# A decoder layer with product-key experts: half of the second-key one-hots on GpSimd, 16 more second-weight passes beside the first weights, a ranking in wider steps

## The chip, the core and the metric

The kernel runs on one core of a Trainium2 chip as one program. The metric is the device time of one execution in microseconds (us). A core has five engines that run their own instruction streams in order and wait for each other by semaphores: TensorE (PE in the profile; PEld is its weight load), VectorE (DVE), ScalarE (ACT), GpSimd (POOL) and SyncE (SP, which here only issues DMAs). DMAs are issued from SP, ACT and POOL, each with a queue of its own; the gathers by index come from POOL.

## What is computed

One layer of a decoder for a prompt of 512 tokens and 8 x 8 sample tokens, with a model width of 2048, in float32. The first half (conditioned norms, an input projection, a gated recurrence and a short convolution, an output projection) isn't touched by the change. The second half is a layer of 16384 single-neuron experts, chosen by product keys:

```python
q = (xb @ w_q).reshape(PEER_BLOCK, PEER_HEADS, 2, HALF_DIM)
sc = jnp.einsum('thpk,pnk->thpn', q, sub_keys)
v1, i1 = lax.top_k(sc[:, :, 0], PEER_TOPK)      # 16 best of 128 first keys
v2, i2 = lax.top_k(sc[:, :, 1], PEER_TOPK)      # 16 best of 128 second keys
cand = v1[..., :, None] + v2[..., None, :]      # 256 pairs
top, pos = lax.top_k(cand, PEER_TOPK)           # 16 of them per head
g = softmax(top)
act = gelu(einsum('td,thkd->thk', xb, expert_u[eidx])) * g
out = einsum('thk,thkd->td', act, expert_v[eidx])
```

With 8 heads each token picks 128 experts. `expert_u` holds the first weights, `expert_v` the second, 16384 rows of 2048 each.

## The kernel before, in words

Experts are grouped by their first key into 128 blocks of 128. A ranking orders the blocks by how often they are picked. For the prompt tokens, the 76 best ranked blocks (L) are computed densely: all 512 tokens against all 128 experts of a block on PE. Picks outside these blocks, and all picks of the sample tokens, are gathered row by row: a POOL DMA fetches 128 expert rows (one per partition, 1 MB) into one of five row buffers (seven in the second stage), and DVE makes one pass over it. A pass in the first-weight stage is a dot product (line 1310); in the second-weight stage it adds the row, weighted, to an accumulator (line 1337). There are 233 passes of the first kind (5 of them copies of token rows) and 228 of the second, in one order; a counter `gu` says how far the passes are, `gf` how far the fetches. Sample rows come first in both halves, as a tile of 64 full gathers; the five tiles of prompt tokens have slots that are left empty.

The work runs in two long stages after the projections.

The first-weight stage has 152 pieces (half a block each, 24 matmuls of 128x512, line 1451). All products are made from a rounded high half and the remainder: ACT makes `xhi` (line 931), POOL `xlo` (line 932), two pieces ahead. Between the pieces, a generator `steps1` (function `choice`) hands out the choosing of the last head, the resolving of indices, a second ranking of the blocks behind the 48th (`rank_rest`), and the sort of the tokens; each step carries a guessed cost, and a balance `spare` says how many are done per piece. When it ends, `steps2` makes the slot lists of one tile of tokens after the other, and gathers of that tile may follow. Alongside, dense weights are built: for each token a matrix of first key by second key, as a product of two one-hots on PE (line 1652, 8 matmuls per 4 tokens). DVE makes the one-hots of 8 tokens in one call (`g_pair`, line 1638: `op` is 128x8x128 for the second key, `wr` 128x8x76 for the first), reading the key row from PSUM; ACT scales each token's `op` by its weight (line 1646). `upto(n)` sets how many must be ready at a piece. `RATE[1]` passes are due per piece while `steps2` runs; then `gather_to` spreads what is left, so that `EARLY_V` passes of the second kind are done when the stage ends.

The second-weight stage has 76 steps of 48 matmuls (line 1471), each with 4 x 0.25 MB of second weights. Every four steps need dense weights (`gsb`, from `gd`) and activations (`actr`), loaded from ACT's queue, multiplied on DVE and split into halves `ahi`, `alo`. The remaining passes are spread over the first 69 steps in proportion to the room that PE's time leaves.

Both stages are recorded by hand in this order (a manual schedule), so the program text fixes each engine's order. PSUM banks of the kind "g" rotate between two: a score, a step of a ranking and a one-hot product that follow each other take turns on them.

Of the kernel before, what the change touches and what calls it, by code (L numbers as in the profile page):

```python
# [10 lines left out]
ALU = mybir.AluOpType  # L11
# [33 lines left out]
LATE = 1  # L45
PIECE = 5.5
BEHIND = 7.0
RATE = (1.0, 2.0)
PIECE_G = 6.9
HEADS_COUNTED = 4  # L50
RANKED = 48
# [1 line left out]
LAG = 4  # L53
FIRST_G = 6
PAIRS = 8
EARLY_V = 8
KEPT = 5
WEIGH = 2.8
PARTS = 2
# [25 lines left out]
def build(ctx, tc, A, O, dbg=None):  # L85
    nc = tc.nc
    V, S, PE, G = nc.vector, nc.scalar, nc.tensor, nc.gpsimd
# [17 lines left out]
    iota = const.tile([128, 128], F32, name="iota")  # L105
# [314 lines left out]
    t0 = c1.tile([128, KW], F32, name="t0")  # L420
# [19 lines left out]
    o = big.tile([128, KD, T], F32, name="o", tag="big")  # L440
# [419 lines left out]
    for i in range(RB):  # L860
        r, k = new_row(f"row0_{i}")
# [691 lines left out]
    late = list(range(QT))  # L1553
    it, stg, pair, puts = [], {}, {}, []

    def choice():
# [5 lines left out]
        picked, rest = iter(()), rank_rest()  # L1562
        yield None
        for a, z in enumerate(order):
            next(rest, None)
            if a and a + 1 < len(order):
                side[order[a + 1]] = score(h, order[a + 1])
            choose(h, side[z], z)
            yield 6.0
            if z == "S":  # L1570
                for _ in resolve("S", EARLY_S, HD // 2 - EARLY_S):
                    yield 4.0
                yield 1.5
                picked = pick_samples()
            yield next(picked, 0.0)
            yield next(picked, 0.0)
        soft = {}
        for z in late:
            for _ in resolve(z, HD - HB):
                yield 9.5  # L1580
            yield 5.5
            yield next(picked, 0.0)
            soft[z] = softmax(z)
            next(soft[z])
# [35 lines left out]
    gk = {}  # L1620
# [9 lines left out]
    def g_pair(b):  # L1630

        rg = pools["rg"]
        t0 = b * 4
        ops = rg.tile([128, 8, 128], F32, name=f"op{b}", tag="op", bufs=PAIRS // 2)
        wr = rg.tile([128, 8, L], F32, name=f"wr{b}", tag="wr", bufs=PAIRS // 2)
        for out, src, j in ((ops, gk["o"], 1), (wr, gk["w"], 0)):
            n = src.shape[-1]
            V.tensor_tensor(out, src[:, None, :].to_broadcast([128, 8, n]),  # L1638
                            it[j][:, t0:t0 + 8, None].to_broadcast([128, 8, n]), op=ALU.is_equal)
        pair[b], pair[b + 1] = (ops, wr, 0), (ops, wr, 4)  # L1640

    def g_scale(b):

        ops, wr, j0 = pair[b]
        for j in range(4):
            S.activation(ops[:, j0 + j, :], ops[:, j0 + j, :], AF.Copy, scale=it[2][:, b * 4 + j:b * 4 + j + 1])  # L1646

    def g_mm(b):
# [26 lines left out]
    spare, due_g = -BEHIND, 0.0  # L1675
# [14 lines left out]
    for n in range(NU2):  # L1690
# [7 lines left out]
        if R1 is not None:  # L1698
            put(2)
            g_one(n)  # L1700
            if not gk:
                g_start()
            elif gm[0] < min(upto(n), gm[1] + PAIRS - 1):
                g_pair(gm[0])
                gm[0] += 2
                spare -= 2.2
            while gm[2] < gm[3]:
                g_scale(gm[2])
                gm[2] += 1
            gm[3], gm[4] = gm[4], gm[0]  # L1710
# [14 lines left out]
        if not even:  # L1725
# [4 lines left out]
            if since is not None and n > since + 2:  # L1730
                due_g += RATE[R1 is not None] + (0.7 if waits and spare > 4.5 else 0.0)
            g0 = gu[0]
# [5 lines left out]
            if waits:  # L1738
                spare = min(spare, 3.0)
# [62 lines left out]
    for m in range(M):  # L1802
        gi, q, bl, first, final = steps[m]
        n = NU2 + 2 * m
# [4 lines left out]
        for kq in range(KD // VQ):  # L1809
# [16 lines left out]
            k, pv = v_column(n, gi, q, bl, first, final, kq)  # L1826
# [33 lines left out]
    with tc.If(any_ > 0), tc.tile_pool(name="fb", bufs=1) as fp:  # L1860
        io1 = fp.tile([128, 128], F32, name="f_io1")
        V.tensor_scalar(io1, iota, 1.0, None, op0=ALU.add)
        for i, (p0, n, c) in enumerate(GT):
# [9 lines left out]
            w = kk[:, 1, :]  # L1873
# [9 lines left out]
            a = fp.tile([128, D], F32, name=f"f_a{i}", tag="a", bufs=1)  # L1883
# [105 lines left out]
```

## Time and profile before

| what | us |
|---|---|
| median of 3 runs | 3182.85 (3177.85 to 3182.97) |
| profiled execution | 3185.91 |
| its span, first to last instruction | 3184.1 |
| first-weight stage (first and last start of its matmuls) | 1183.7 to 2181.5 |
| second-weight stage | 2181.5 to 3159.1 |
| one-hots on DVE | 1518.5 to 2061.7 |
| PE, DVE, POOL, ACT busy | 3006.2, 2129.4, 1762.6, 1021.2 |

Busy shares say little over the whole span, since its stages differ; rows below are taken by stretch of time. A row of instruction groups reads: line, engine, operation, tiles, shapes, count, then busy time, mean duration in ns, and the idle time of that engine just before them, with what ended it. A row of waits reads: who waited, for whom, us in total, times, longest. In the DMA views a line of an issue ends with its count and the median us from issue to landing; a line of a queue has packets, MB and the share of the 16 DMA engines' time. A busy PE is not PE at its peak, since ends of matmuls are modelled.

### The profile page before, as it was taken

The page shows a single profiled execution, that of the slowest core. Times are in us where ns is not written, and L with a number is a line of the kernel's source. Part 1 is how long each engine was busy: PE and PEld are TensorE (multiplying, and loading weights), DVE is VectorE, ACT ScalarE, POOL GpSimd, SP SyncE. Part 2 cuts the span into 40 slices and gives each one's busy share as a digit, 9 for nine tenths or more (in the row PEclk, how much of TensorE's full clock was granted, in tenths as well). Part 3 has the DMA queues.
Part 4 walks back from the last instruction along what each step waited for, and adds up shares of the span by engine and source line. Part 5 has one row for each costly group of instructions (what it writes and reads, how often), then busy time and mean ns, then how long its engine had stood idle before and what let it go on. Part 6 is the DMA issues. An engine that isn't in the chain of part 4 may idle for free. (4 is left out here: it accounts for less than half of the span.)

```text
span 3184.1 us, 46037 instructions
## 1 busy us (share of the span) xinstructions
PE 3006.2 (94%) x16954; PEld 2550.9 (80%) x16954; DVE 2129.4 (67%) x3301; ACT 1021.2 (32%) x1619; POOL 1762.6 (55%) x1071
## 2 busy tenths in 40 slices
PE   6999999999999999999999999997999898989797
PEld 2788888889989997887888888875888676767576
DVE  3455521142246899987998999966577687769755
ACT  3244311122232232222656655622322121112122
POOL 2233333344334235667566666667888686878662
PEclk9999999999999999999999999998999999999898
DMA  9744566533332127889879999999999998899984
GB/s 394 279 138 137 178 214 216 205 122 131 128 118 102 68 81 258 309 305 391 311 309 368 420 369 409 403 367 379 381 400 406 381 340 324 326 363 364 368 305 146
DMA packets 292071, 892.40 MB, mean 280 GB/s; under 512 B 35776, under 2 KB 75584, under 8 KB 237664
## 3 DMA queue, kind: packets, MB, share of 16 engines
q0 software_dynamic: 67776, 435.61, 34.3%
q1 hardware_dynamic: 157152, 372.00, 32.5%
q10 hardware_dynamic: 66912, 81.81, 7.4%
q8 instruction: 134, 2.20, 0.3%
q14 instruction: 97, 0.79, 0.1%
HBM read 879.89 MB, written 64.71 MB: 297 GB/s over the span
## 5 line engine op out<-in xcount | busy, mean ns | idle before, releaser
L932 POOL TENSOR_TENSOR xlo<-raw,xhi 128x1024 fp32r<-128x1024 f32 x304 | 738.7, 2441 | 324.2 <-ACT xhi L931 233.1
L1337 DVE SCALAR_TENSOR_TENSOR accB<-v,dots,accB 128x2048 f32<-128x2048 f32 x216 | 508.2, 2353 | 214.3 <-DMA v<-v,rows 213.1
L931 ACT ACTIVATE xhi<-raw 128x1024 fp32r<-128x1024 f32 x304 | 318.3, 1058 | 883.7 <-PE pv L1471 251.7
L1310 DVE SCALAR_TENSOR_TENSOR u<-u,hT 128x2048 f32<-128x2048 f32 x228 | 515.3, 2281 | 98.6 <-DMA u<-u,rows 98.1
L1471 PE MATMUL pv<-ahi,xhi 128*128 128x512 f32 x1216 | 491.2, 404 | 62.1 <-ACT xhi L931 47.3
L1471 PE MATMUL pv<-ahi,xlo 128*128 128x512 f32 x1216 | 487.8, 401 | 14.6 <-POOL xlo L932 14.5
L1451 PE MATMUL pu<-hhi,xhi 128*128 128x512 f32 x1216 | 492.8, 405 | 3.7 <-ACT xhi L931 3.7
L1471 PE MATMUL pv<-alo,xhi 128*128 128x512 f32 x1216 | 488.7, 402 | 5.9 <-POOL alo L1426 5.9
L1451 PE MATMUL pu<-hhi,xlo 128*128 128x512 f32 x1216 | 480.6, 395 | 7.1 <-POOL xlo L932 7.1
L1451 PE MATMUL pu<-hlo,xhi 128*128 128x512 f32 x1216 | 478.9, 394 | 0.0
L1282 POOL DMA_INDIRECT u<-u,rows x228 | 232.0, 1018 | 231.1 <-DVE u L1310 171.5
L1471 PEld LDWEIGHTS pv<-ahi,xhi 128*128 128x128 f32 x1216 | 233.7, 192 | 124.8 <-ACT xhi L931 52.6
L1471 PEld LDWEIGHTS pv<-ahi,xlo 128*128 128x128 f32 x1216 | 233.1, 192 | 75.6 <-POOL xlo L932 21.2
L1471 PEld LDWEIGHTS pv<-alo,xhi 128*128 128x128 f32 x1216 | 233.2, 192 | 60.0 <-POOL alo L1426 7.6
L1282 POOL DMA_INDIRECT v<-v,rows x228 | 248.5, 1090 | 58.2 <-issue 37.3
L1451 PEld LDWEIGHTS pu<-hhi,xlo 128*128 128x128 f32 x1216 | 230.1, 189 | 62.0 <-POOL xlo L932 9.8
L1451 PEld LDWEIGHTS pu<-hhi,xhi 128*128 128x128 f32 x1216 | 230.6, 190 | 50.3 <-ACT xhi L931 4.5
L1451 PEld LDWEIGHTS pu<-hlo,xhi 128*128 128x128 f32 x1216 | 231.1, 190 | 46.1
L1646 ACT ACTIVATE op<-op,it 128x128 f32<-128x128 f32 x512 | 155.6, 389 | 31.6 <-DVE op L1638 31.2
L132 POOL TENSOR_TENSOR wlo_o<-raw_o,whi_o 128x1024 fp32r<-128x1024 f32 x32 | 77.5, 2423 | 119.9 <-ACT whi_o L130 119.9
L1652 PEld LDWEIGHTS gbank<-wr,op 128*128 128x128 f32 x1024 | 133.7, 191 | 12.6 <-ACT stg L1659 2.6
L132 POOL TENSOR_TENSOR wlo_q<-raw_q,whi_q 128x1024 fp32r<-128x1024 f32 x28 | 67.2, 2402 | 132.3 <-ACT whi_q L130 132.3
(515 smaller groups left out, 5542.9 us busy)
## 6 DMA issues: line engine op xcount, KB each, us to landing
wa<-w_ada SPq DMA_DIRECT2D x96, 1024.0 KB, 7.4
raw<-ut SPq DMA_DIRECT2D x152, 512.0 KB, 7.9
raw<-v SPq DMA_DIRECT2D x304, 256.0 KB, 10.1
actd<-act ACTq DMA_DIRECT2D x76, 256.0 KB, 7.6
gd<-stg ACTq DMA_DIRECT2D x64, 304.0 KB, 12.8
gsb<-gd ACTq DMA_DIRECT2D x76, 256.0 KB, 17.0
actr<-actd ACTq DMA_DIRECT2D x38, 512.0 KB, 9.4
raw_o<-w_out SPq DMA_DIRECT2D x32, 512.0 KB, 3.6
```

The lines of the kernel that those rows point to most:

```text
L132: lo_engine(share).tensor_sub(lo, raw, r32(hi))
L931: S.activation(hi, raw, AF.Copy)
L932: G.tensor_sub(lo, raw, r32(hi))
L1282: G.indirect_dma_start(out=out, out_offset=None, in_=src, in_offset=bass.IndirectOffsetOnAxis(ap=idx, axis=0), bounds_check=NE * 128 - 1, ...
L1310: V.scalar_tensor_tensor(r, r, 1.0, st["h"], op0=ALU.mult, op1=ALU.mult, accum_out=dots[i][:, j:j + 1])
L1337: V.scalar_tensor_tensor(st["a"], r, dots[i][:, j:j + 1], st["a"], op0=ALU.mult, op1=ALU.add)
L1451: PE.matmul(pu, st[:, kk, :], movA[mv](k), start=k == 0 and a == 0, stop=k == KD - 1 and a == 2)
L1471: PE.matmul(pv, st, mv, start=first and j == 0 and a == 0, stop=last and not end and j == SG - 1 and a == 2)
L1646: S.activation(ops[:, j0 + j, :], ops[:, j0 + j, :], AF.Copy, scale=it[2][:, b * 4 + j:b * 4 + j + 1])
L1652: PE.matmul(pg[:, j * L:(j + 1) * L], ops[:, j0 + j, :], wr[:, j0 + j, :], start=True, stop=True)
```

## The change

Three things, by the diff.

One-hots: of the eight tokens of a pair call, POOL makes `op` for the first four, comparing and scaling in one instruction per token (four tensor_scalars of 128x128 with two per-partition operands); DVE makes `op` for the other four and `wr` for all eight; ACT scales only the other four.

Passes: `EARLY_V` goes from 8 to 24, `RATE[1]` from 2.0 to 2.2, and a pair's guessed cost from 2.2 to 1.6, so that steps of `steps2` are handed out a little earlier.

Second ranking: its three steps came with the first three tiles of `choice`; now the first comes with the second tile, the second with the fourth, the third with the first `resolve`.

```diff
-RATE = (1.0, 2.0)
+RATE = (1.0, 2.2)
-EARLY_V = 8
+EARLY_V = 24
...
         for a, z in enumerate(order):
-            next(rest, None)
+            if a in (1, 3):
+                next(rest)
             if a and a + 1 < len(order):
                 side[order[a + 1]] = score(h, order[a + 1])
...
         for z in late:
+            if z in late[:2]:
+                next(rest, None)
             for _ in resolve(z, HD - HB):
...
-        for out, src, j in ((ops, gk["o"], 1), (wr, gk["w"], 0)):
+        for j in range(4):
+            G.tensor_scalar(ops[:, j, :], iota, it[1][:, t0 + j:t0 + j + 1], it[2][:, t0 + j:t0 + j + 1],
+                            op0=ALU.is_equal, op1=ALU.mult)
+        for out, src, j, k in ((ops, gk["o"], 1, 4), (wr, gk["w"], 0, 0)):
             n = src.shape[-1]
-            V.tensor_tensor(out, src[:, None, :].to_broadcast([128, 8, n]),
-                            it[j][:, t0:t0 + 8, None].to_broadcast([128, 8, n]), op=ALU.is_equal)
+            V.tensor_tensor(out[:, k:], src[:, None, :].to_broadcast([128, 8 - k, n]),
+                            it[j][:, t0 + k:t0 + 8, None].to_broadcast([128, 8 - k, n]), op=ALU.is_equal)
...
-        for j in range(4):
+        for j in range(4 if j0 else 0):
             S.activation(ops[:, j0 + j, :], ops[:, j0 + j, :], AF.Copy, scale=it[2][:, b * 4 + j:b * 4 + j + 1])
...
-                spare -= 2.2
+                spare -= 1.6
```

Where instructions move, on PE in the middle of the seventh piece of the first-weight stage (`rk` is a bank of the ranking, `sc` one of scores, `pu` the piece's products). Before:

```order
L1451 MATMUL pu_11803<-hhi,xlo_11681 128x512
L976 MATMUL rk_11837<-rk_low,rowi 128x128
L761 MATMUL sc_7_11841<-keys,qt_11276 128x128
L761 MATMUL sc_7_11841<-keys,qt_11395 128x128
L761 MATMUL sc_7_11871<-keys,qt_11276 128x128
L761 MATMUL sc_7_11871<-keys,qt_11395 128x128
L1451 MATMUL pu_11803<-hhi,xhi_11752 128x512
```

and of the change:

```order
L1451 MATMUL pu_11795<-hhi,xlo_11673 128x512
L761 MATMUL sc_7_11829<-keys,qt_11276 128x128
L761 MATMUL sc_7_11829<-keys,qt_11395 128x128
L968 MATMUL rk_11860<-ident,rk_row 128x128
L761 MATMUL sc_7_11867<-keys,qt_11276 128x128
L761 MATMUL sc_7_11867<-keys,qt_11395 128x128
L1451 MATMUL pu_11795<-hhi,xhi_11744 128x512
```

The last matmul of the ranking (line 976) stood between two scores' turns of the banks; now its first step's transpose (line 968) does, and line 976 stands alone, about four pieces later.

On POOL, in the stretch of the one-hots, for the same tile of tokens (`xlo` is a remainder for PE, `u` a gather). Before:

```order
L932 TENSOR_TENSOR xlo_16119<-raw_16043,xhi_16118 128x1024
L1282 DMA u_9_16139<-u,rows_8709 128x2048
L1282 DMA u_10_16144<-u,rows_8709 128x2048
L932 TENSOR_TENSOR xlo_16180<-raw_16113,xhi_16179 128x1024
L1282 DMA u_11_16208<-u,rows_8709 128x2048
L1282 DMA u_12_16213<-u,rows_8709 128x2048
```

and of the change:

```order
L1640 TENSOR_SCALAR op_16040<-iota,it_13513,it_13514 128x128 x4
L1282 DMA u_9_16048<-u,rows_8709 128x2048
L1282 DMA u_10_16053<-u,rows_8709 128x2048
L932 TENSOR_TENSOR xlo_16089<-raw_16023,xhi_16088 128x1024
L1640 TENSOR_SCALAR op_16099<-iota,it_13513,it_13514 128x128 x4
L1282 DMA u_11_16111<-u,rows_8709 128x2048
L1282 DMA u_12_16116<-u,rows_8709 128x2048
L1282 DMA u_13_16121<-u,rows_8709 128x2048
```

Four tensor_scalars stand between a remainder and the gathers of most pieces, and every fifth piece has three gathers where it had two.

## The prediction

> **What bounds the kernel now.** I read busy time by stretches first, with edges where something changes: the stall of the ranking (1227), the one-hots (1480), the tail of the first-weight stage (2060 to 2182), and in the second-weight stage the place where stalls set in (2467). Columns are the row of names; the last three are granted clock, DMA share and GB/s.
>
> ```profile
> core 0: us, PE busy (x) PEld busy (x) DVE busy (x) ACT busy (x) POOL busy (x), PEclk, DMA share, GB/s
> 1227.00:1245.00 18.00, 10.29 (x40) 8.46 (x39) 17.00 (x65) 1.71 (x3) 5.02 (x4) 0.72 0.60 217
> 1480.00:1690.00 210.00, 209.86 (x1069) 177.19 (x1067) 185.27 (x306) 116.87 (x255) 130.28 (x86) 1.00 0.83 325
> 1690.00:2060.00 370.00, 367.29 (x1937) 312.37 (x1938) 348.61 (x452) 223.79 (x500) 232.85 (x160) 1.00 0.98 398
> 2060.00:2182.00 122.00, 112.68 (x491) 90.98 (x491) 81.36 (x63) 31.79 (x43) 81.12 (x52) 0.96 0.96 368
> 2222.00:2467.00 245.00, 245.00 (x1057) 198.49 (x1056) 170.40 (x97) 64.75 (x64) 202.87 (x128) 1.00 1.02 395
> 2467.00:3062.00 595.00, 523.97 (x2161) 413.32 (x2160) 443.38 (x258) 114.81 (x106) 444.86 (x291) 0.94 0.93 349
> ```
>
> To see: from 1480 to 2060 PE never stops, so the first-weight stage is as long as its matmuls. In the second-weight stage a step is 48 matmuls: 22 steps in 245 us, 11.1 each with PE full, then 45 steps in 595 us, 13.2 each. Those 45 hold 45 x 2.1 = 94 us of stalls, the largest loss here. The DMA views of these two stretches, then the waits of the second, say what sets that pace.
>
> ```profile
> DMA packets 33370, 96.85 MB, mean 395 GB/s; under 512 B 2830, under 2 KB 13328, under 8 KB 25603
> v<-v,rows POOLq DMA_INDIRECT x61, 11.0
> ...
> DMA packets 74865, 207.81 MB, mean 349 GB/s; under 512 B 9765, under 2 KB 32035, under 8 KB 58142
> q0 software_dynamic: 22486, 136.73, 57.6%
> gsb<-gd ACTq DMA_DIRECT2D x41, 256.0 KB, 22.9
> v<-v,rows POOLq DMA_INDIRECT x149, 11.7
> ```
>
> ```profile
> DVE accB L1337 <- DMA v<-v,rows: 147.7, 80, 12.5
> ACT xhi L931 <- issue: 111.2, 11, 25.2
> ACT xhi L931 <- DMA raw<-v: 101.0, 20, 19.9
> ACT xhi L931 <- DMA gsb<-gd: 69.6, 6, 22.2
> ```
>
> DVE waits for gathered rows, ACT for weights (gsb) and for its own DMA issues, POOL stands behind both, and PE gets its halves late: the stretch is bound by transfers. A step carries 96.85 / 22 = 4.40 MB in the early stretch, which PE's pace still allows, and 207.81 / 45 = 4.62 MB in the late one, which it doesn't.
>
> **The change part by part.** *The 16 moved passes.* In program order 152 passes stand behind the 24th step now, 139 then; the first 24 steps give up only 3, where PE is full anyway: nothing there. Behind them 13 gathers of 136.73 / 149 = 0.92 MB leave, 11.9 MB of 207.81. At the stretch's own 349 GB/s that is 34 us; counted in engine share (57.6% x 595 / 149 = 2.3 us each, 30 us, over the share of 0.93) 32 us. That is the low end of the gain. The high end: 195.9 / 45 = 4.35 MB a step is just under the 4.40 that ran at 11.1 us; a step's share falls from 0.93 x 13.2 = 12.3 to 11.6 us, and at the early share of 1.02 it takes 11.4 us, 45 x 1.8 = 82 us less. I take 48: nearer to the low end, since 111 us of ACT's waits are its own issues and gsb takes 22.9 us to land, and such chains shrink no faster than the traffic beside them.
>
> *What the 16 cost in the first-weight stage.* Four more gathers run before 1690, at 325 GB/s and under a full PE: free. About ten more fall into 1690 to 2060, two into the tail.
>
> ```profile
> GB/s 257 370 421 425 418 424 420 420 421 419 420 421 420 422 418 407 358 262 250 381 420 424 423 420 420 419 426 415 424 423 416 357 275 379 423 417 422 422 417 418
> DMA packets 32276, 147.16 MB, mean 398 GB/s; under 512 B 4769, under 2 KB 4769, under 8 KB 20095
> q0 software_dynamic: 15086, 99.81, 65.2%
> u<-u,rows POOLq DMA_INDIRECT x104, 13.1
> ```
>
> That is the DMA view of 1690 to 2060: most of its 40 slices stand at 420 GB/s, a ceiling. 147.16 MB at 421 would need 349.5 us, so 20.5 us are free, all in the two dips. Ten gathers of 0.96 MB take 22.8 us at the ceiling: 2 us beyond the room if the dips fill, 23 if they can't (they stand where a new tile of slots starts). I take 12. The tail: two full gathers, 2.1 MB at 368 GB/s, 6 us, since PE already stalls there. Together +18.
>
> In sentences of its own: the Trainium skill (SBUF — State Buffer, "A bandwidth-pool intuition that's wrong (but worth ruling out)") puts a core's share of HBM at about 358 GB/s and calls HBM nearly always the end-to-end bottleneck. By that the first-weight stage could take nothing more, and the change would give nothing. The 420s above disagree with it here.
>
> *DVE's relief.* Rows by form, the one-hots' line, and POOL's and DVE's waits in 1690 to 2060 (the x104 row and the one behind it):
>
> ```profile
> L1638 DVE TENSOR_TENSOR op<-kb,it x64: 1206/1219/1221, 1518.5 to 2060.6; 128x1024 f32<-128x1024 f32 x64
> L1310 DVE SCALAR_TENSOR_TENSOR u<-u,hT 128x2048 f32<-128x2048 f32 x164 | 370.8, 2281 | 54.6 <-DMA u<-u,rows 54.4
> L1646 ACT ACTIVATE op<-op,it 128x128 f32<-128x128 f32 x512 | 155.6, 389 | 31.6 <-DVE op L1638 31.2
> L1282 POOL DMA_INDIRECT u<-u,rows x104 | 103.7, 997 | 133.0 <-DVE u L1310 99.6 <-PE gbank L1652 10.3 <-PE pu L1451 6.2
> DVE u L1310 <- DMA u<-u,rows: 18.9, 19, 1.8
> L932 POOL TENSOR_TENSOR xlo<-raw,xhi 128x1024 fp32r<-128x1024 f32 x304 | 738.7, 2441 | 324.2 <-ACT xhi L931 233.1 <-issue 70.0 <-DMA raw<-v 16.9
> L1426 POOL TENSOR_TENSOR alo<-actr,ahi 128x512 fp32r<-128x512 f32 x76 | 97.2, 1313 | 1.2 <-ACT ahi L1421 0.4
> L284 POOL TENSOR_TENSOR ms_h<-ms_h,mod 128x256 f32<-128x256 f32 x4 | 4.0, 1007 | 3.9 <-DVE mod L214 3.9
> L106 POOL IOTA iota<- 128x128 f32 x1 | 0.2, 235 | 0.4 <-POOLq L1980 0.4
> ```
>
> Half a one-hot is 0.61 us, over 64 pairs 39 us; 16 more passes at 2.3 us are 37 us. DVE, 94% busy there, stays where it is, and only therefore can it feed the faster gathers. ACT's 256 scalings fewer (0.39 us each) gain nothing: PE covers ACT.
>
> *POOL's new work.* 256 tensor_scalars of 128x128, of a kind that the trace doesn't show. Low end: the 128x128 iota, 0.235 us, which reads nothing. High end: 1.007 us, the 128x256 product with a broadcast operand. The line through 1024 and 512 elements (2.44 and 1.31 us: 2.2 ns an element, 0.19 fixed) gives 0.47 at 128; I take that, one input against two, but two scalar pointers. In 1690 to 2060 PE's row of one-hot matmuls has
>
> ```profile
> 1690.00:2060.00 370.00, 85.56 (x677) 88.31 (x678) 1.00 0.98 398
> ```
>
> 677 / 2 tokens, so 42 pairs and 169 of the new instructions: 80 us, and 10 for the gathers, against 370 - 232.85 = 137 us in which POOL is idle, 99.6 of them waiting for DVE to free a row. Cost nothing while one takes under (137 - 10) / 169 = 0.75 us. Behind them on POOL stand the next gathers and the next xlo, for which PE waits; without that cover every 0.1 us more is 17 us in this stretch. Their own wait, for a buffer that PE's matmuls release, is one that DVE's first one-hot had before, and it idled 0.0 us.
>
> A rule that speaks against this, in sentences of its own: the skill's page SBUF — State Buffer, "Who interferes with whom", says a VectorE instruction with two SBUF inputs and a GpSimd one that reads SBUF block each other for their whole length. The same DVE form at 1178.9, beside an xlo, and at 1184.6 alone agrees:
>
> ```profile
> 1178.90 2.23 DVE L775 SCALAR_TENSOR_TENSOR cnt<-s,cnt 128x128 f32<-128x128 f32 x1
> ...
> 1184.61 0.26 DVE L775 SCALAR_TENSOR_TENSOR cnt<-s,cnt 128x128 f32<-128x128 f32 x1
> ```
>
> But the first row of DVE's block above is flat from 1206 to 1221 ns beside a POOL busy 63%: one-hots and dot products take one input from PSUM. By the rule only the slot lists' short operations are left to collide; the sum keeps its value.
>
> *The second ranking.* PE's one long wait of the early stage:
>
> ```profile
> PE sc L761 <- DVE perm L977: 7.7, 1, 7.7
> ...
> 1220.86 2.27 DVE L1310 SCALAR_TENSOR_TENSOR u<-u,hT 128x2048 f32<-128x2048 f32 x1
> ...
> 1236.52 0.28 DVE L977 COPY perm<-rk 128x128 f32<-128x128 f32 x1
> ```
>
> A score needs the bank of the ranking's last matmul, which DVE empties at 1236.5, behind three dot products. In the new order that matmul comes four pieces later with no score behind it; the score that stands there instead, at the same place near 1228, needs what DVE does right behind the dot product of 1220.9, over by 1225. The gain lies between 0 (DVE, 17 of 18 us busy there, then stands 8 us further behind, and another wait appears) and 9 (the stretch's 40 matmuls at 245 / 1057 us are 9.3 of its 18). I take 8: it is PE's only wait named before 1480.
>
> **Sum.** -48 + 18 + 0 + 0 - 8 = -38. The profiled execution took 3185.91 us (span 3184.1), 3.1 above the median of the runs, 3182.85. So 3147.9 for such an execution, 3145 by the median.
>
> **Rivals.** *Second stage at PE's pace*: -82, +18, -8 = -72, 3111. For it: 4.35 MB a step is below what ran stall-free. Against: ACT's issue waits.
> *One ceiling for both stages*: the dips don't fill (+29), the late stretch gives 32, and the ranking's 8 us are lost in waiting for transfers: -3, 3180. For it: 420 GB/s at 13 us to land from 1690 on; against: 325 before it.
> *POOL becomes the bound (slower)*: a tensor_scalar at 1.0 us instead of 0.47. In 1690 to 2060 169 x 0.25 = 42 us beyond the room; in 1480 to 1690 the other 87 take 87 us, where 80 are idle: 7. Gathers and xlo queue behind it and lose as much again where both miss their turn: +98, against -56 and the +18: +60, 3243. It decides from 0.75 us on; level with now at about 0.86. For it: POOL runs 63% there and two pointers are untried; against: the line through two sizes.
> *The move does less than it says*: the stall at 1227 only turns into another, with the rest as forecast: -30, 3153.
>
> **How the numbers follow.** Forecast 0.45 (its own range 3125 to 3165), PE's pace 0.16, one ceiling 0.18, POOL 0.15, no gain from ranking 0.06. A measurement of this kernel tells 0.2%, 6.4 us, from no change. Faster: 0.45 + 0.16 + 0.06 and a quarter of one ceiling, 0.72. Same: half of it and a little of POOL, 0.11. Slower: the rest, 0.17. The range runs from 3108, below PE's pace, to 3193, a POOL that costs a little more than it gives; beyond it lie most of POOL's case and a few hundredths below.
>
> **What would show it.** The wait of sc for perm gone and 1227 to 1245 about 8 us shorter. op tensor_scalars under 0.75 us, POOL near 85% from 1690 to 2060, and its wait for u falling from 99.6 to some 30. DVE one-hots at 0.61. DVE's wait for u rows up from 18.9; the first-weight stage ending 5 to 15 us later than 2182. Steps behind the 24th near 12.2 us, their GB/s at 350 to 375, gsb landing below 22.9. I am wrong if these steps still take 13 us, or if the first-weight stage grows by more than 40.

## The result, and the profile after

The changed kernel takes 3219.91 us, the median of 4 runs (3211.72 to 3225.05), against 3182.91 for the kernel before, timed beside it: a ratio of 1.0115, 95% interval 1.0089 to 1.014. It is slower by 37 us where the forecast was 38 us faster, and above the range's upper end of 3193. The profiled execution took 3225.05 us, its span 3223.0 (before: 3185.91 and 3184.1).

I first put both traces on one scale: the 152 pieces of the first-weight stage are 24 matmuls each, so the start of every 24th matmul of `pu` dates a piece, and the first matmul of `pv` ends the stage. All times in us, from one execution each.

| | before | after | difference |
|---|---|---|---|
| start of the first-weight stage | 1183.9 | 1186.0 | +2.1 |
| pieces 0 to 55 (ranking, slot lists begin) | 333.3 | 338.5 | +5.2 |
| pieces 56 to 135 (one-hots) | 560.6 | 624.5 | +63.9 |
| pieces 136 to 151 and the turn (tail) | 103.9 | 111.1 | +7.2 |
| second-weight stage to the end | 1002.4 | 962.8 | -39.6 |
| span | 3184.1 | 3223.0 | +38.9 |

Most of the gain that the passes were to bring is there. The loss lies nearly whole in the pieces with one-hots, which the forecast had held at PE's own length. Busy time by stretches of the kernel after, cut like the forecast's (one-hots begin, one-hots, tail, the second-weight stage up to its 24th step, and the 45 steps behind it):

```profile
core 0: us, PE busy (x) PEld busy (x) DVE busy (x) ACT busy (x) POOL busy (x), PEclk, DMA share, GB/s
1524.00:1707.00 183.00, 170.56 (x877) 142.06 (x876) 155.90 (x256) 79.51 (x153) 169.27 (x152) 0.99 0.76 290
1707.00:2149.00 442.00, 409.48 (x2064) 340.12 (x2064) 365.16 (x478) 183.67 (x350) 399.00 (x356) 0.97 0.94 373
2149.00:2260.00 111.00, 97.18 (x395) 76.53 (x395) 68.84 (x40) 22.90 (x27) 71.26 (x48) 0.92 0.99 383
2300.00:2544.00 244.00, 244.00 (x1053) 197.41 (x1052) 167.83 (x94) 64.19 (x64) 198.12 (x124) 1.00 1.02 389
2544.00:3102.00 558.00, 516.45 (x2165) 410.86 (x2164) 430.42 (x246) 115.23 (x107) 433.19 (x282) 0.96 0.93 349
```

To see: from 1524 to 2149 POOL is now 91% busy (169 and 399 of 183 and 442 us), DVE 83%, and PE, which idled 3 us in the same pieces before, idles 45 us and is granted 0.97 to 0.99 of its clock. The lower clock costs some 15 us more by an estimate from these rows, (1 - 0.97) x 442 + (1 - 0.99) x 183; together that is most of the 64 us. In the last row 2165 matmuls are 45.1 steps: 12.4 us each, for 13.2 before and 12.2 forecast. The DMA view of that stretch has 194.85 MB for 207.81, at the 349 GB/s of before, and the weights that ACT waited for landing in 19.0 us, 22.9 before:

```profile
DMA packets 73775, 194.85 MB, mean 349 GB/s; under 512 B 9741, under 2 KB 32161, under 8 KB 58768
...
gsb<-gd ACTq DMA_DIRECT2D x41, 256.0 KB, 19.0
```

The groups of POOL and DVE by form have the new rows:

```profile
L1640 POOL TENSOR_SCALAR op<-iota,it,it 128x128 f32<-128x128 f32 x256 | 201.6, 794 | 0.0
...
L1644 DVE TENSOR_TENSOR op<-kb,it 128x512 f32<-128x512 f32 x64 | 43.8, 685 | 0.0
```

One weighted one-hot takes POOL 0.794 us. The sum had taken 0.47 and called everything below 0.75 free. Who waits, between 1707 and 2149 (us in total, times, longest):

```profile
ACT xhi L931 <- DMA raw<-ut: 89.6, 24, 9.1
DVE u L1310 <- DMA u<-u,rows: 72.4, 57, 4.9
...
PE gbank L1658 <- ACT stg L1665: 16.3, 10, 2.5
PE pu L1451 <- POOL xlo L932: 16.0, 9, 3.5
POOL u L1282 <- DVE u L1310: 14.0, 18, 2.5
```

POOL no longer waits for DVE to free a row (99.6 us in the like stretch before, 14.0 now). It is late itself, and a circle stands behind it: an xlo that comes late frees its raw buffer late, so the next weights are loaded late, and ACT waits for them. SP, which issues these loads, waits for xlo between 1524 and 2100, before and after:

```profile
SPq L915 <- POOL xlo L932: 470.0, 82, 14.7
```

```profile
SPq L915 <- POOL xlo L932: 505.7, 74, 14.2
```

A wait is 6.8 us in the mean where it was 5.7; that each turn of the circle delays the next is read from these rows and wasn't tested apart. PE stops for xlo, and for ACT's eviction of the one-hots' bank.

### The profile page after: what moved, and what is told of

The parts are those of the page before. It is cut to its first block, busy times and chain, and to the rows that moved or that the text cites. A ratio compares the mean times of both kernels' runs of the same rounds, so it can differ in the third digit from the quotient of the medians.

```text
span 3223.0 us, 46036 instructions
## 1 busy us (share of the span) xinstructions
PE 3024.5 (94%) x16954; PEld 2555.9 (79%) x16954; DVE 2134.2 (66%) x3301; ACT 944.6 (29%) x1363; POOL 1962.7 (61%) x1327
## 5 line engine op out<-in xcount | busy, mean ns | idle before, releaser
L1451 PE MATMUL pu<-hhi,xlo 128*128 128x512 f32 x1216 | 489.6, 403 | 38.1 <-POOL xlo L932 38.0
L1451 PE MATMUL pu<-hhi,xhi 128*128 128x512 f32 x1216 | 499.3, 411 | 7.2 <-ACT xhi L931 7.2
L1282 POOL DMA_INDIRECT v<-v,rows x228 | 240.3, 1054 | 67.8 <-issue 36.7
L1640 POOL TENSOR_SCALAR op<-iota,it,it 128x128 f32<-128x128 f32 x256 | 201.6, 794 | 0.0
L1658 PE MATMUL gbank<-wr,op 128*128 128x76 f32 x1024 | 131.7, 272 | 20.4 <-ACT stg L1665 20.2
```

What stands on the lines that cost most here:

```text
L1282: G.indirect_dma_start(out=out, out_offset=None, in_=src, in_offset=bass.IndirectOffsetOnAxis(ap=idx, axis=0), bounds_check=NE * 128 - 1, ...
L1451: PE.matmul(pu, st[:, kk, :], movA[mv](k), start=k == 0 and a == 0, stop=k == KD - 1 and a == 2)
L1640: G.tensor_scalar(ops[:, j, :], iota, it[1][:, t0 + j:t0 + j + 1], it[2][:, t0 + j:t0 + j + 1], op0=ALU.is_equal, op1=ALU.mult)
L1658: PE.matmul(pg[:, j * L:(j + 1) * L], ops[:, j0 + j, :], wr[:, j0 + j, :], start=True, stop=True)
```

## The experiments

Sixteen kernels ran. Three questions: which part of the change costs what; whether the moved passes are paid in DVE's time or in transfers; and where POOL's price begins to count. This table has the stages of all of them, dated as above; the sections below give edits and readings.

| kernel | first-weight stage | pieces 56 to 135 | tail | second-weight stage | median |
|---|---|---|---|---|---|
| before | 997.8 | 560.6 | 103.9 | 1002.4 | 3182.9 |
| after | 1074.2 | 624.5 | 111.1 | 962.8 | 3219.9 |
| ranking alone | 1002.2 | 560.2 | 104.4 | 993.8 | 3189.9 |
| passes alone | 1052.8 | 587.6 | 131.7 | 953.9 | 3203.7 |
| POOL's one-hots alone | 1032.9 | 590.0 | 108.7 | 996.9 | 3215.1 |
| passes and ranking | 1056.7 | 589.9 | 128.8 | 970.5 | 3211.2 |
| ACT's one-hots alone | 1011.0 | 572.0 | 104.8 | 996.8 | 3195.2 |
| ACT's, passes, ranking | 1048.2 | 600.5 | 110.0 | 960.9 | 3197.3 |
| ACT's, passes | 1045.2 | 600.1 | 110.9 | 962.4 | 3196.3 |
| POOL's at 0.60 us | 1002.0 | 569.1 | 98.6 | 990.3 | 3191.6 |
| two of eight on POOL | 1002.7 | 565.7 | 102.7 | 999.8 | 3188.8 |
| before, POOL's forms at the start | 1000.1 | 560.9 | 104.7 | 1002.3 | |
| half dots, 8 / 24 passes | 994.0 / 1042.6 | 557.1 / 581.2 | 106.6 / 131.0 | 1004.6 / 961.3 | |
| half u rows, 8 / 24 | 979.8 / 1002.6 | 556.5 / 557.2 | 89.1 / 111.1 | 994.4 / 975.9 | |
| half u and v rows, 8 / 24 | 980.0 / 996.1 | 556.5 / 557.1 | 89.1 / 104.0 | 903.0 / 903.8 | |

The kernels without a median ran once. Executions of one kernel lie up to some 25 us apart, and a row here is one execution. The pieces repeat well: 56 to 135 take 560.6, 560.2 and 560.9 us in the three kernels with the same work there. The second-weight stage doesn't: it ranges from 990.3 to 1002.4 over the six whole kernels with 8 passes. So a few us are read from the pieces, and only 15 or more from the second-weight stage.

One thing decides which rows may be compared. The pair's guessed cost, which came with the passes in the change, goes with the one-hots in these kernels, and it settles where the moved gathers stand. In POOL's timelines, gathers ahead of the remainder of a piece, against the kernel before:

| kernels | guessed cost | passes | piece 80 | piece 136 | first step of the second-weight stage |
|---|---|---|---|---|---|
| the change; ACT's with passes (both) | 1.6 | 24 | 0 | +12 | +16 |
| passes alone, with ranking, with half dots or rows | 2.2 | 24 | 0 | +4 | +15 |
| one-hots alone (POOL's in all three forms, ACT's) | 1.6 | 8 | 0 | -3 | 0 |

The change puts 12 of its 16 gathers into the pieces with one-hots, the kernel with the passes alone only 4, and the rest into its tail.

**The parts one by one.** The change without POOL's one-hots (DVE makes all eight again, ACT scales them):

```diff
-        for j in range(4):
-            G.tensor_scalar(ops[:, j, :], iota, it[1][...], it[2][...], op0=ALU.is_equal, op1=ALU.mult)
-        for out, src, j, k in ((ops, gk["o"], 1, 4), (wr, gk["w"], 0, 0)):
+        for out, src, j in ((ops, gk["o"], 1), (wr, gk["w"], 0)):
...
-        for j in range(4 if j0 else 0):
+        for j in range(4):
             S.activation(...)
...
-                spare -= 1.6
+                spare -= 2.2
```

> The changed kernel with the one-hots of all eight tokens back on VectorE and the scalings back on ScalarE; the 24 early passes and the spread ranking stay. Theory POOL (the tensor_scalars at 0.794 us fill GpSimd and hold up the halves and the gathers): the one-hot pieces lose most of their 64 us again, but VectorE, 94% busy there before, now has some 10 more passes of 2.3 us in that stretch, 23 us, which it can't hide; 3183 - 40 (second-weight stage) + 25 to 40: 3160 to 3185. Theory GATHERS (the 16 more gathers in the first-weight stage are what costs 64 us, whoever makes the one-hots): the first-weight stage stays at about 1074 us, 3215 to 3235.

Measured: 3211.2, ratio 1.0077 (1.0055 to 1.0098). Neither theory's range, and nearer to GATHERS: with POOL as free as before, the first-weight stage is still 59 us longer. But with the cost of 2.2 most of the moved gathers go into the tail, which takes 128.8 us where the change's takes 111.1. So this is not the change without POOL's work and nothing else; what POOL costs is read from the next kernel.

The kernel before with POOL's one-hots alone (the inverse of the diff above, applied to it):

> The kernel before with GpSimd's one-hots alone; 8 early passes and the old ranking. Theory POOL: the first-weight stage grows by 40 to 65 us and nothing is won behind it: 3223 to 3248. Theory GATHERS: no more gathers, so no growth, and VectorE has half of the one-hots' 1.2 us off: 3170 to 3185.

Measured: 3215.1, ratio 1.0087 (1.0064 to 1.011). The stage grew by 35 us, 29 of them in pieces 56 to 135, with no gather added and DVE relieved: POOL costs by itself, though the total came out 8 us below the theory's range.

The kernel before with the second ranking spread alone:

```diff
-            next(rest, None)
+            if a in (1, 3):
+                next(rest)
...
+            if z in late[:2]:
+                next(rest, None)
```

> The kernel before with the second ranking spread out and nothing else. Theory EATEN (the 9 us gained in two pieces come back as waits of a later piece, where GpSimd's gather waits for VectorE and the halves stand behind it): 3179 to 3186, the long wait of a score for the ranking gone, a piece some ten pieces later 5 to 7 us longer. Theory GAIN (the later long pieces come from the other parts of the change): 3172 to 3177.

Measured: 3189.9, ratio 1.0018 (1.0005 to 1.0031): EATEN, and a little more than eaten: 4 us above that range. The score's wait for the ranking is gone and pieces 0 to 15 took 96.1 us for 105.5. Then piece 16 took 12.1 us for 5.4 and three between 41 and 46 together 6 longer, so that the 56 pieces together took 337.5 us for 333.3. The timelines of POOL and of PE at piece 16 (start, length, instruction, the idle time before it and who ended it) show how:

```profile
1281.74 1.00 POOL L1282 DMA_INDIRECT u<-u,rows  x1 [7.95 <-DVE u L1310]
...
1282.77 2.38 POOL L932 TENSOR_TENSOR xlo<-raw,xhi 128x1024 fp32r<-128x1024 f32 x1
```

```profile
1280.92 0.39 PE L1451 MATMUL pu<-hhi,xhi 128*128 128x512 f32 x1
1281.14 0.39 PE L1451 MATMUL pu<-hlo,xhi 128*128 128x512 f32 x1
1285.19 0.80 PE L1451 MATMUL pu<-hhi,xlo 128*128 128x512 f32 x1 [3.66 <-POOL xlo L932]
1285.79 0.63 PE L1451 MATMUL pu<-hhi,xhi 128*128 128x512 f32 x1
1286.21 0.63 PE L1451 MATMUL pu<-hlo,xhi 128*128 128x512 f32 x1
...
1290.48 0.63 PE L1451 MATMUL pu<-hhi,xlo 128*128 128x512 f32 x1
```

A gather waits 8 us on POOL for a row that DVE hasn't freed yet, the xlo behind it is late, PE stops for 3.7 us, and then its matmuls start 0.43 us apart instead of 0.23 until 1290.9. Busy time of the same stretch, before and with the ranking spread:

```profile
1183.90:1290.00 106.10, 98.39 (x452) 81.10 (x451) 102.29 (x302) 32.33 (x40) 59.71 (x33) 0.95 0.70 247
```

```profile
1184.80:1290.00 105.20, 100.86 (x462) 82.63 (x461) 101.68 (x283) 33.62 (x41) 58.23 (x33) 0.97 0.68 248
```

DVE is busy 102 of some 106 us in both. It sets this stretch, and PE's wait at the old place was only where its backlog showed; there it cost a score, here a weight half.

The kernel before with the passes alone:

```diff
-RATE = (1.0, 2.0)
+RATE = (1.0, 2.2)
-EARLY_V = 8
+EARLY_V = 24
```

> The kernel before with 24 early second-weight passes at the quicker pace, nothing else. If the parts add up: the run with ranking and passes together, 3211, less the 7 us of the ranking alone: 3202 to 3207. Theory VECTOR (94% busy in the one-hots before, it has no room for the added passes of 2.3 us, and the first-weight stage grows by about 50 us): its pieces with long matmul gaps stand where VectorE's dot products run without a pause. Theory TRANSFERS (420 GB/s is the ceiling): VectorE then waits for gathered rows for at least 50 us more than before in that stretch.

Measured: 3203.7, ratio 1.0073 (1.0046 to 1.01), as the parts add up. The passes cost the first-weight stage 55 us and give the second 48.5 in the traced execution, which is the fastest of five (3193.5). The two signs that were to tell VECTOR from TRANSFERS didn't: of the waits in 1524 to 2100, DVE's for rows grew only from 46.2 us to

```profile
DVE u L1310 <- DMA u<-u,rows: 60.1, 64, 2.3
ACT xhi L931 <- DMA raw<-ut: 51.4, 20, 9.0
```

while ACT's for first weights, the second row, had been 15.3. The transfers' own rows say more. Gathers and bytes from 1184 to 1700, before:

```profile
DMA packets 35648, 158.40 MB, mean 307 GB/s; under 512 B 5612, under 2 KB 5612, under 8 KB 23664
...
u<-u,rows POOLq DMA_INDIRECT x105, 9.9
```

and with the passes:

```profile
DMA packets 35456, 157.69 MB, mean 306 GB/s; under 512 B 5576, under 2 KB 5576, under 8 KB 23489
...
u<-u,rows POOLq DMA_INDIRECT x103, 9.6
```

The quicker pace brought nothing forward while there was room: in the order of every kernel here 103 gathers stand ahead of the 80th remainder, since a gather has to follow the slot list of its tile. And second-weight gathers issued from 1184 to 2237, before and with the passes:

```profile
v<-v,rows POOLq DMA_INDIRECT x21, 9.2
```

```profile
v<-v,rows POOLq DMA_INDIRECT x22, 11.9
```

At 2237, where the second-weight stage begins with the passes, as many of its gathers have been issued as in the kernel before at that same time. In the clock's time the "earlier" passes are not earlier; the stage's matmuls only start later, with more passes behind them.

By the DMA views the tail moves 49.0 MB for 37.3, which is 28 us at 420 GB/s, and it takes 28 us longer. Pieces 56 to 135 move only 209.6 MB for 207.5, 5 us at that rate, and take 27 longer. There the order has changed: in eight of the 56 pieces behind the 80th no gather stands in POOL's order, where it was three, and in others three instead of two. The pace and the number of passes were never changed apart, so how these 27 us split between them stays open.

**DVE or transfers?** ACT instead of POOL makes the four weighted one-hots, so DVE is relieved as in the change and POOL has nothing to do for it:

```diff
-            G.tensor_scalar(ops[:, j, :], iota, it[1][...], it[2][...], op0=ALU.is_equal, op1=ALU.mult)
...
+                S.activation(o, iota, AF.Abs, bias=it[1][:, t:t + 1], scale=-1.0)
+                S.activation(o, o, AF.Relu, bias=it[2][:, t:t + 1], scale=it[3][...])   # it[3] holds -it[2]
```

With the passes and the spread ranking:

> The changed kernel with the four weighted one-hots made by ScalarE (the distance of the key from the row's index by Abs, then Relu of weight minus weight times distance, two instructions for a token) and none on GpSimd; VectorE makes half as in the change; 24 passes and the spread ranking stay. Theory POOL AND VECTOR (each half of the growth comes from an engine that was filled): both have room now, the one-hot pieces grow by no more than 20 us, the second-weight stage keeps its gain of 40: 3150 to 3172. Theory TRANSFERS (the added gathers themselves cost the 50 us): 3190 to 3212.

Measured: 3197.3, ratio 1.0044 (1.0027 to 1.006). TRANSFERS. With 8 passes and the old ranking:

> The kernel before with ScalarE's one-hots alone: 8 early passes and the old ranking. VectorE is relieved of 0.6 us a pair and gets nothing in its place. Theory POOL AND VECTOR: TensorE had no stall in the one-hots before, so nothing is won there, and at most some 10 us in the tail: 3172 to 3184. If ScalarE's four more instructions of 0.39 us a pair make the halves late, 3190 or more.

Measured: 3195.2, ratio 1.0042 (1.0026 to 1.0058): the last case; PE waits for ACT's evictions (20 times, 8.0 us, beside 1.3 before) and pieces 56 to 135 are 11 us longer. With the passes and the old ranking:

> ScalarE's one-hots and the 24 early passes with the old ranking. Theory POOL AND VECTOR: the run with ScalarE's one-hots and both other parts, less 4 to 7 us for the ranking: 3145 to 3168, faster than the kernel before. Theory TRANSFERS: 3185 to 3205.

Measured: 3196.3, ratio 1.0043 (1.0026 to 1.0061): TRANSFERS again. On top of ACT's own 11 us the passes cost pieces 56 to 135 28 us, on top of DVE's one-hots 27, on top of POOL's 34: relieving DVE buys nothing there. ACT's pair of kernels differs by the passes alone and has the change's own order of gathers, so it prices them best. The transfers in these 80 pieces without and with the passes:

```profile
DMA packets 47786, 207.63 MB, mean 363 GB/s; under 512 B 8029, under 2 KB 8029, under 8 KB 31225
```

```profile
DMA packets 49874, 218.87 MB, mean 365 GB/s; under 512 B 8721, under 2 KB 8721, under 8 KB 31967
```

11.2 MB more take 28 us more, 401 GB/s. The first-weight stage is 34.2 us longer, the second 34.4 shorter, and the medians, 3195.2 and 3196.3, are the same: moved, and nothing won. Since ACT's load is a disturbance of its own, I then took away DVE's work and the bytes directly, each with 8 and with 24 passes and nothing else changed. Half dot products (the sums leave out half of each row):

```diff
-            V.scalar_tensor_tensor(r, r, 1.0, st["h"], op0=ALU.mult, op1=ALU.mult, accum_out=...)
+            V.scalar_tensor_tensor(r[:, :D // 2], r[:, :D // 2], 1.0, st["h"][:, :D // 2], ...)
```

> Control with VectorE relieved: the kernel before, each first-weight dot product over half of its row (1024 of 2048 columns, so some 1.2 us for 2.28; the transfers stay whole). Its first-weight stage may shrink a little from 998 us; what counts is its difference to the next kernel.

> The same half dot products with the 24 early passes at the quicker pace. With whole dot products the passes lengthened the first-weight stage by 55 us (27 in the pieces with one-hots, 28 in the tail). Theory VECTOR (its lag holds up GpSimd's gathers, and the halves behind them): here 0 to 12 us against the control. Theory TRANSFERS (the 420 GB/s are the wall): still 40 to 60.

Half of the first-weight rows (the upper half of the experts isn't fetched, and the dot products are zero):

```diff
-            take(held[j][0], A["u"], rows_i[i][:, j:j + 1])
+            take(held[j][0], A["u"], rows_i[i][:, j:j + 1], NE * 64)   # bounds_check = NE * 64 - 1
...
-            V.scalar_tensor_tensor(r, r, 1.0, st["h"], ...)
+            V.scalar_tensor_tensor(r, r, 0.0, st["h"], ...)
```

> Control with the transfers relieved: the kernel before, with the first-weight gathers of the upper half of the rows skipped (about half of their bytes; as many instructions on GpSimd and VectorE, dot products times zero). Its first-weight stage may shrink a little from 998 us; what counts is its difference to the next kernel.

> The same half of the gathered bytes with the 24 early passes at the quicker pace. Theory VECTOR: the first-weight stage is still 40 to 60 us longer than the control's. Theory TRANSFERS: 0 to 12 us.

Measured: with half dot products the passes still lengthen the stage by 49 us, as TRANSFERS has it; with half rows by 23, between the two ranges, of which 0.7 us in pieces 56 to 135. From 1700 to 2100, the kernel before; passes alone; then with half dots and 24 passes; then with half rows and 24:

```profile
1700.00:2100.00 400.00, 397.46 (x2081) 337.64 (x2080) 366.44 (x459) 231.60 (x509) 254.75 (x174) 1.00 0.99 401
```

```profile
1700.00:2100.00 400.00, 387.32 (x2005) 325.90 (x2004) 358.64 (x474) 231.13 (x515) 240.26 (x167) 0.99 0.95 382
```

```profile
1700.00:2100.00 400.00, 388.79 (x2026) 327.16 (x2025) 250.49 (x471) 229.34 (x510) 242.21 (x169) 0.99 0.97 390
```

```profile
1700.00:2100.00 400.00, 400.00 (x2099) 340.65 (x2098) 368.03 (x461) 231.22 (x511) 261.53 (x181) 1.00 0.84 300
```

DVE's load falls from 359 to 250 us in the third row, and PE still stands for 11 us (13 with whole dot products). In the fourth DVE is as full as ever (368), the engines of the transfers are down to 0.84, and PE never stops. In the one-hot pieces the passes' cost goes with the bytes of the rows and not with DVE's work, shown from both sides in the order of the passes alone. The 22 us that were left in the tail, where second-weight rows are fetched, were tested with half of those skipped too (the same bound in the second-weight gathers):

> Control: the kernel before with the gathers of the upper half of the rows skipped for both weights (about half of the gathered bytes; dot products times zero). The second-weight stage should lose most of its 94 us of stalls if transfers bind it; its first-weight stage is the one to compare with the next kernel's.

> The same with the 24 early passes at the quicker pace. Theory TRANSFERS: the tail of the first-weight stage, 22 us longer with whole second-weight rows, grows by at most 8 us. Theory VECTOR in the tail (2.45 passes a piece of 5.5 us at 2.3 us each leave VectorE no time): still 15 to 25 us.

Measured: the tail grew from 89.1 to 104.0, by 15 us, where TRANSFERS was to leave at most 8 and VECTOR 15 to 25. PE, which never waits in the control's tail, waits 7.8 us here, four times for xlo and twice for xhi, and its clock is at half for 13.7 us, some 7 us more. That doesn't settle the cause. Half of the added rows' bytes are still fetched, 32.8 MB for 26.4, which is 15 us at 420 GB/s; but the tail's mean is 315, with the transfers' engines at 0.90. Two waits of this run between 2060 and 2200 point at the activations' weighting, which DVE does behind the added passes:

```profile
ACT xhi L931 <- POOL alo L1426: 14.8, 1, 14.8
ACT ahi L1421 <- DVE actr L1414: 10.9, 1, 10.9
```

That chain was not taken apart further. The second-weight stage, in turn, is 903.0 and 903.8 us with 8 and 24 passes: with half of the gathered bytes gone its 100 us of stalls go, and with them all that moving passes can win.

**From where on does POOL's work cost?** The kernel before with four of each form of POOL instruction at the program's start, results unused:

> The kernel before with four each of several GpSimd instructions at the program's start, on a constant tile, their results unused; only their durations count. Theory POINTERS (the 0.794 us are a start-up that the two per-partition scalars add): two scalars from memory on 128x128 0.79 us, one 0.5 to 0.65, none 0.3 to 0.47, and 128x512 with two at 1.5 to 1.9. Theory ELEMENTS (a dearer element): 128x512 with two at 2.4 to 3.0 us, 64 columns at 0.4 to 0.5, and nothing gained with scalars in the instruction.

POOL's groups by form (`two`, `t`: comparison and product with two scalars from memory; `one`: comparison with one; `i`: with a constant; `bsub`: a subtraction of two broadcast operands):

```profile
L129 POOL TENSOR_SCALAR mb_t<-mbf,mbc 128x512 f32<-128x512 f32 x4 | 8.3, 2082 | 0.0
...
L129 POOL TENSOR_SCALAR mb_i<-mbf 128x512 f32<-128x512 f32 x4 | 6.0, 1502 | 0.0
...
L129 POOL TENSOR_SCALAR mb_t<-mbf,mbc 128x256 f32<-128x256 f32 x4 | 4.9, 1224 | 0.0
...
L136 POOL TENSOR_TENSOR mb_bsub<-mbf 128x512 f32<-128x512 f32 x4 | 4.2, 1050 | 0.0
...
L129 POOL TENSOR_SCALAR mb_two<-mbf,mbc 128x128 f32<-128x128 f32 x4 | 3.2, 790 | 0.5 <-DVE mbc L115 0.5
...
L129 POOL TENSOR_SCALAR mb_one<-mbf,mbc 128x128 f32<-128x128 f32 x4 | 2.4, 594 | 0.0
L129 POOL TENSOR_SCALAR mb_t<-mbf,mbc 128x64 f32<-128x64 f32 x4 | 2.3, 582 | 0.0
...
L134 POOL TENSOR_TENSOR mb_sub<-mbf 128x128 f32<-128x128 f32 x4 | 1.9, 468 | 0.0
L139 POOL COPY mb_copy<-mbf 128x128 f32<-128x128 f32 x4 | 1.2, 296 | 0.0
```

Both theories miss. From 64 to 512 elements the weighted form grows by 1.50 us, 3.35 ns an element on 0.37 us fixed; from 0.594 to 0.790 is what the second operation and its scalar add. The element is dear, and the start-up is not small. The line that the forecast drew through two sizes of a subtraction was right for a subtraction (0.468 measured, 0.47 forecast); it was the wrong row for a tensor_scalar. The Trainium skill (GPSIMD Engine Reference, 4.1 Engine selection) calls one-input operations on GpSimd roughly line-rate and two-input ones about twice as slow as VectorE; here a one-input comparison with a constant took 1.50 us at 128x512, more than the 1.05 of the two-input subtraction beside it, so the measurement decides. It is the tensor_scalar that is dear and not the single input: a copy of 128x128 took 0.296 us, the subtraction 0.468.

So the same four one-hots at the price of one operation, and ACT scaling all eight:

```diff
+            G.tensor_scalar(ops[:, j, :], iota, it[1][:, t0 + j:t0 + j + 1], None, op0=ALU.is_equal)
```

> The kernel before with four of eight unweighted one-hots on GpSimd (one comparison with one scalar from memory, 0.594 us in the run of forms) and all eight scalings on ScalarE; 8 passes, old ranking. With weighted ones at 0.794 the first-weight stage grew by 35 us. Theory THRESHOLD (free below 0.75 us): it grows by no more than 8 us, 3180 to 3190. Theory ANY WORK (GpSimd's halves and gathers wait for whatever is put ahead of them): it grows in the measure of the work, 35 x 0.594 / 0.794 = 26 us, 3203 to 3212.

and the weighted ones for two tokens of eight:

```diff
+        for j in range(2):
+            G.tensor_scalar(ops[:, j, :], iota, it[1][...], it[2][...], op0=ALU.is_equal, op1=ALU.mult)
```

> The kernel before with two of eight weighted one-hots on GpSimd at 0.794 us, the other six as before. Theory THRESHOLD (1.6 us a pair, well below the 3.0 that four at 0.75 would take): the first-weight stage within 5 us of 998, 3178 to 3188. Theory ANY WORK: half of the 35 us, 3196 to 3204.

Measured: 3191.6, ratio 1.004 (1.0023 to 1.0057), and 3188.8, ratio 1.002 (1.0004 to 1.0037). The first-weight stage grew by 4 and 5 us, as THRESHOLD has it; the medians are slightly above its ranges. The traced execution of the first (3177.0) is its fastest of seven, so its row of stages is on the low side. Busy time from 1700 to 2100 with POOL's one-hots at 0.794, at 0.60, and with two of eight:

```profile
1700.00:2100.00 400.00, 384.28 (x1981) 322.67 (x1980) 321.67 (x413) 177.46 (x339) 372.99 (x331) 0.98 0.95 369
```

```profile
1700.00:2100.00 400.00, 394.49 (x2060) 332.19 (x2059) 340.97 (x427) 227.90 (x510) 349.64 (x337) 1.00 0.98 394
```

```profile
1700.00:2100.00 400.00, 395.43 (x2078) 334.50 (x2076) 351.78 (x432) 211.20 (x436) 321.38 (x256) 1.00 0.99 396
```

POOL at 93, 87 and 80% (63% in the forecast's stretch of before); pieces 56 to 135 longer by 29, 8.5 and 5 us. There is no clean threshold in these three, which have one order of gathers. The price creeps in with the load and climbs steeply between 87 and 93%. The guessed cost of 1.6 wasn't run alone; what it costs is inside the 5 us of the last.

None of these kernels beat the one before; each of the change's three parts is, alone, a loss, the ranking's 0.2% the least certain of them.

## Why the prediction was wrong, point by point

- **The 16 moved passes behind the 24th step, -48: right in kind, too large.** The pair of traces has -39.6, of which 38 in the 45 late steps; the pairs with the same one-hots and order have -34; over the five kernels with 24 passes the stage is 962.1 us in the mean, over the six whole kernels with 8 it is 996.7, 35 less. That is near the low bound of 32, and by its rule: the bytes went down as forecast (194.85 MB, 195.9 forecast) and the rate stayed at 349 GB/s, so a late step takes 12.4 us and not 12.2. That the gathered bytes bind the stage is shown by the runs with half the rows of both weights: a late step takes 11.2 us there.
- **Their cost in the first-weight stage, +18: wrong, 34 to 37 in the change's own order** (on top of ACT's and of POOL's one-hots, the ranking's 4 us left out) and 55 in the order of the passes alone. The step that failed is "four more gathers run before 1690, at 325 GB/s and under a full PE: free", and with it the room in the dips. Nothing moved ahead of the 80th piece: 103 gathers by 1700 instead of 105, though the pace was raised. So all 16 fall behind it, and each costs nearly its whole transfer: 16 x 0.96 MB at 420 GB/s are 37 us. The dips didn't fill either (365 GB/s over ACT's 80 pieces, 363 without the passes). The rival with one ceiling had this mechanism; it priced it at +29 in the stage and had the ranking cancel.
- **The tail, +6: 2 to 6 in the change's order, 28 with the passes alone.** The difference is where the gathers stand: 4 of the 16 in the tail of the change, 12 with the passes alone. What the tail waits for when its added rows are halved stays open.
- **DVE's relief, 0: right in sum, for the wrong reason.** Half a one-hot block takes 0.685 us, not half of 1.22, and the relief fed no faster gathers: DVE's halved dot products took 3.5 us off pieces 56 to 135. That POOL's work beside them would hold up DVE's long operations, which the forecast weighed and set aside, doesn't show: between 1524 and 2100 a dot product took 2.281 us before and 2.284 after, a `wr` one-hot 0.779 and 0.780.
- **POOL's new work, 0: wrong, the largest error: 32 us when it is made alone** (3215.1 for 3182.9). 0.794 us instead of 0.47, taken from the line through two sizes of a two-operand subtraction. And the rule put on it, free below 0.75 us, would have made 0.794 cost only (0.794 - 0.75) x 169 = 7 us; 29 were measured in pieces 56 to 135 alone. Adding up idle time failed too: the 137 us in which POOL stood idle were not all usable. The likely reason, not tested, is that the work comes in bursts of four in a queue in which an xlo must not be late.
- **The second ranking, -8: wrong, 4 us lost in 56 pieces.** The bound of nothing was argued in the same paragraph, since DVE was busy 17 of 18 us there. Taking 8 because it was PE's only named wait mistook the place of the stall for its cause. The low bound should have gone below nothing: the stall came back at a worse place.
- **The rivals.** POOL as the bound had the right sign at a price of 1.0 us; at 0.794 its own arithmetic gave a gain, so it was right in kind only. One ceiling for both stages was the other half. I had priced them as alternatives, and the change met both: in the pieces with one-hots POOL's work cost 29 us alone, and the passes on top of it 34 more, the 64 measured.
- **Together.** Forecast: 0 for POOL, -30 for the passes, -8 for the ranking. Measured: +32 for POOL, about 0 for the passes (34 won, 34 to 37 lost), +4 for the ranking in its pieces: some +37. The forecast's own sign of being wrong, a first-weight stage longer by more than 40 us, came true with 76.

## What to carry to other kernels

When a stage runs at the transfers' ceiling, moving transfers into it from another that does moves the stall and wins nothing (34 us each way here); look at what has been issued by one and the same time of the clock, before and after, and at where the order of the program lets the moved ones stand. An operation that the trace doesn't show is priced from its own form (its number of operations and scalars), not from another instruction with fewer inputs, and the idle time of an in-order engine that feeds the bound one can't just be added up: POOL at 80, 87 and 93% cost 5, 8.5 and 29 us here. A stall behind which an engine was busy all the while is that engine's: reordering moves it.

## What the runs showed of the hardware

- A POOL tensor_scalar with two operations and two scalars from memory: 0.58, 0.79, 1.22 and 2.08 us for 64, 128, 256 and 512 columns. With one operation and a constant 512 columns took 1.50; a subtraction of two broadcast operands over 512 columns took 1.05, half of the weighted comparison.
- A short stall of PE costs more than its length: after 3.66 us without a matmul at 1285.2 they started 0.43 us apart instead of 0.23 for 5.7 us, so that the piece lost 6.7 us. The trace's granted clock is 0.50 through that time. The kernel after has ten such stretches between 1240 and 2150, eight of 3.4 us and two of 6.8. Ahead of each, two starts on PE lie 2.1 to 4.1 us apart; 16 other gaps, of 1.3 to 3.1 us, have none behind them. The Trainium skill (TensorE: Matmul & The Clock Gate, Part 1: The HAM clock gate) has the array go to half rate after an idle window of about 3.4 us and back after as long a busy one. The lengths of the stretches agree, one window or two. The condition doesn't: eight of the ten gaps are shorter than the window, and the measurement decides. What tells these from the 16 isn't shown here.
- The 420 GB/s of the transfers stand as a wall on this one busy core: of the 40 slices between 1700 and 2100 in the kernel before none passes 426. The Trainium skill (HBM Reference, Specifications (TRN2)) gives about 425 GB/s for a core that streams alone, bounded by its 16 DMA engines, and agrees.
